# A hybrid retention and attention step: first loads into the key and score buffers, the last head's rows later, new delays

## The chip, the cores and the metric

The kernel runs on one core of one Trainium2 chip. The metric is the device time of one execution in microseconds (us); lower is better. The version before the change takes 669.69 us, the median of three runs (669.68, 669.69 and 672.77).

## The reference, cut to what matters

One step of a layer for 1024 prompt tokens and 64 sample tokens (the sample tokens have a cache of 128 keys and a running retention state), width 1024:

```python
h = rmsnorm(x, norm_g)
z = h @ w_in                        # 4096 columns: q, k, v, gate of 8 retention and 4 differential heads
o_ret  = retention(rotate(rq), rotate(rk), rv)       # per-token causal, a state per head
p = softmax(q_c @ k_c.T, masked)    # c = 0, 1, for each differential head, rotary on a part of q and k
o_diff = (p[0] - lam * p[1]) @ dv   # keys of the own and earlier 64-token chunks
mix = concat(rmsnorm(o_ret) * g * silu(rg), rmsnorm(o_diff) * g * (1 - lam0) * silu(dg))
y = final_rmsnorm(x + mix @ w_out)
# returned: y, the retention states, and k and v of the differential heads
```

## The kernel before, in words

**Tiles and groups.** The tokens are nine tiles: tiles 0 to 7 of 128 prompt tokens, tile 8 of 64 sample tokens. The input projection is cut into eight groups of 512 columns, in the order R0, D0, R1, D1, R2, D2, R3, D3: an R group holds q, k, v and gate of two retention heads, a D group those of one differential head. For each group, `proj` (L277) makes one 128x512 product `z` per tile; the first group takes tiles 0 to 3 together. Then `outproj` (L666) makes the two halves `zo0` and `zo1` of the output projection, tile by tile, adds x, and the final norm follows.

**Split precision.** x and the weights are each split in two parts, x = xh + xl and w = hi + lo. For each of the eight slices of 128 rows (k = 0 to 7) a tile takes three matmuls of 512 columns: xh with hi, xl with hi, xh with lo (tile 8: two). ScalarE writes the first part by a copy (`xh` L185, weights L138), VectorE the second by a subtraction (`xl` L186, weights L147). A weight slice lies in one of 12 slots (`WRING`, tag wsp), a raw one in one of 3 (`WRAW`, tag wraw), which the x rows for the norm (`xk`) and the rows of y share.

**How x comes in.** The transposed x of tiles 0 to 3 comes as eight slices `x0_k` of 256 KB, each for all four tiles (L226 to 232), through a ring of two buffers with the tag xraw; the loop asks for slice k, then has it split, so that SP, the DMA queue's engine, waits for a split before it asks for the slice after the next. Tiles 4 to 8 come as two halves each of 256 KB through the same ring (`load_x` L198, `prep_x` L205), each asked for and split while the group before that tile runs. `prep_ss` (L218) squares and sums the rows `xk` for the norm. Tag p is the ring of three 4 KB-wide score buffers of the differential heads; `khh` and `kll` hold a differential head's keys in two parts, and a differential head's first use of them is in the second group.

**What sets the order.** TensorE runs in the order in which the program emits it. A clock `clk.t` (in ns) adds up an estimate for each matmul. The steps after a projection (`diff_post` L328, `ret_post` L470) are generators that are cut into steps: each yield gives a delay (`D_QK`, `D_SPLIT`, ...), `HOLD[(group, tile, step)]` adds to it, and `pump` (L589) emits, after each k of a projection, the steps whose time `clk.t` has passed and whose buffers are counted free. `PACE_L` spaces the tiles of the last D group. The other engines' order is the scheduler's, which follows the order of the program and of what is ready. A D tile's steps: transposes `T`, the splits `qs`, `khh`, `kll`; scores `s` for c = 0, then 1 with row maxima `nm` (VectorE L410) and exponentials `p` (ScalarE L415); transposes `wt` of the combined weights and the copy `wT` (L444, L446), both for two halves of the keys where a tile has more than four blocks; the products `o`; a sum of squares (L181, L182, L462), the scaled product `mx` (VectorE L464); its transpose `mt` (L111); the copy `mix` (ScalarE L322). An R tile has `T`, the copies `rkT`, `rqT`, `qpad` (ScalarE L512), scores `s` and the masked `at` (VectorE L520), `o`, `mx` (VectorE L553), `mt`.

**The turn to the output projection.** Rows of groups 0 to 6 go to DRAM and come back (`prep_mix` L647, buffers `mraw`), three tiles ahead. The rows of the last group are split from `mix` itself by `prep_last` (L658), which forces all steps that are still missing for that tile. It is called one tile ahead: before the projection of tile i starts, the rows of tile i + 1 are forced out.

## Time and profile before

| | |
|---|---|
| median of the runs | 669.69 us |
| the profiled execution's own time | 671.67 us |
| its span in the trace | 669.9 us |
| granted TensorE clock, mean | 0.999 |
| TensorE matmuls busy | 649.4 us (97%) |
| VectorE busy | 462.9 us (69%) |
| ScalarE busy | 370.8 us (55%) |
| GpSimd busy | 91.2 us (14%) |

The span runs from the first to the last instruction that the profiler saw; 1.8 us of the execution's time lie outside it. PE is the matmul side of TensorE, PEld its weight loads, DVE is VectorE, ACT ScalarE, POOL GpSimd. In a timeline a row gives start, duration, engine, source line, operation, output <- inputs, shape, count, and in brackets the idle time of the engine just before it with the instruction whose end released it. Matmuls overlap, so a matmul's own duration is longer than the step from one start to the next. A row of the view by windows gives, for one stretch of time, the busy time of each engine.

### The profile page before, as it was taken

The numbers are of one execution on the slowest core, as the hardware profiler recorded it, in microseconds if no ns is written. First come the engines' busy times: TensorE is split into PE (matmuls) and PEld (weight loads), VectorE is DVE, ScalarE is ACT, GpSimd is POOL, SyncE is SP. The second block draws the span as 40 slices with busy tenths as digits, with TensorE's granted clock in tenths as the row PEclk, the third lists the DMA queues.
The fourth block names the chain that finished last, engine by engine and source line by source line (L and its number), as shares of the span: only waits on it lengthen the run. The fifth ranks groups of instructions, "written<-read, shape, count | busy, mean of one in ns | idle before, by whom it ended". The sixth has DMA issues, their size and how long they took to land.

```text
span 669.9 us, 10635 instructions
## 1 busy us (share of the span) xinstructions
PE 649.4 (97%) x3360; PEld 536.9 (80%) x3360; DVE 462.9 (69%) x1486; ACT 370.8 (55%) x1259; POOL 91.2 (14%) x194
## 2 busy tenths in 40 slices
PE   9989999999999999999999999999999998989996
PEld 7867878888888888788888788887887786778885
DVE  5487777797757566877676669766677788864533
ACT  6586565655546555654465557554655566742322
POOL 1222211001221011011111110111210100010000
PEclk9999999999999999999999999999999999999999
DMA  7973410230004101400022004000251025424464
GB/s 241 302 245 111 133 31 20 76 103 16 9 21 140 30 9 48 141 1 25 8 86 92 15 23 156 20 8 18 80 166 43 9 86 152 130 95 140 128 212 165
DMA packets 41192, 59.17 MB, mean 88 GB/s; under 512 B 6896, under 2 KB 25072, under 8 KB 41136
## 3 DMA queue, kind: packets, MB, share of 16 engines
q1 hardware_dynamic: 40848, 58.22, 27.4%
q8 instruction: 27, 0.44, 0.3%
q14 instruction: 29, 0.24, 0.1%
q10 hardware_dynamic: 288, 0.27, 0.1%
HBM read 42.91 MB, written 15.56 MB: 87 GB/s over the span
## 4 chain that ended last, share of the span: by engine, by line
PE 59%; DVE 16%; DMA 9%; ACT 8%; issue 4%; POOL 4%; SPq 0%; POOLq 0%; ACTq 0%; DVEq 0%
PE z L107 34%; PE zo L107 9%; PE s L107 8%; PE o L107 3%; POOL ss L182 3%; DMA wr<-in_wg 2%; DVE nm L410 2%; ACT p L415 2%; PE wt L111 2%; DMA x<-in_x 2%; PE T L111 2%; DVE kll L387 2%; DVE ws L147 1%; DVE xl L186 1%; DMA wr<-in_wo 1%
## 5 line engine op out<-in xcount | busy, mean ns | idle before, releaser
L107 PE MATMUL z<-ws,xh 128*128 128x512 f32 x1152 | 404.9, 409 | 0.5 <-ACT xh L185 0.5
L107 PEld LDWEIGHTS z<-ws,xh 128*128 128x128 f32 x1152 | 215.9, 189 | 41.1 <-ACT xh L185 1.0
L107 PE MATMUL z<-ws,xl 128*128 128x512 f32 x512 | 200.5, 392 | 0.4 <-DVE xl L186 0.4
L182 POOL TENSOR_TENSOR ss<-ss,m 128x2 f32<-128x2 f32 (+1 forms) x72 | 50.0, 694 | 459.6 <-DVE ss L181 453.3
L107 PEld LDWEIGHTS z<-ws,xl 128*128 128x128 f32 x512 | 97.0, 190 | 12.4 <-DVE xl L186 0.7
L415 ACT ACTIVATE p<-s,nm 128x384 f32<-128x384 f32 (+4 forms) x104 | 58.4, 565 | 73.0 <-DVE nm L410 41.6
L107 PE MATMUL zo<-ws,xh 128*128 128x512 f32 (+1 forms) x304 | 92.5, 384 | 0.0
L107 PEld LDWEIGHTS zo<-ws,xh 128*128 128x128 f32 x304 | 56.2, 189 | 10.3 <-ACT zo L693 0.2
L138 ACT ACTIVATE ws<-wr,early 128x512 fp32r<-128x512 f32 x80 | 54.2, 721 | 13.2 <-PE zo L107 4.6
L410 DVE TENSOR_REDUCE nm<-s 128x1 f32<-128x384 f32 (+4 forms) x104 | 55.7, 537 | 6.4 <-PE s L107 4.8
L147 DVE SCALAR_TENSOR_TENSOR ws<-wr,early,ws 128x512 fp32r<-128x512 f32 x80 | 57.6, 740 | 2.8 <-ACT ws L138 2.2
L387 DVE TENSOR_TENSOR kll<-T,khh 64x128 fp32r<-64x128 f32 (+1 forms) x144 | 40.3, 280 | 17.3 <-ACT khh L385 15.4
L107 PE MATMUL zo<-ws,xl 128*128 128x512 f32 (+1 forms) x136 | 51.3, 377 | 0.0
L107 PEld LDWEIGHTS o<-v,wT 128*128 128x128 f32 x288 | 39.1, 191 | 9.1 <-DVE mx L464 2.8
L107 PE MATMUL o<-v,wT 128*128 128x128 f32 x288 | 40.4, 276 | 3.3 <-DVE mx L464 2.4
L553 DVE SCALAR_TENSOR_TENSOR mx<-s,ss,gt 128x64 f32<-128x64 f32 x72 | 17.2, 280 | 35.7 <-POOL ss L549 35.6
L107 PE MATMUL s<-khh,qs 128*128 128x384 f32 (+4 forms) x104 | 36.8, 354 | 0.0
L107 PE MATMUL s<-kll,qs 128*128 128x384 f32 (+4 forms) x104 | 34.9, 339 | 0.3 <-DVE kll L387 0.2
L322 ACT ACTIVATE mix<-mt 128x128 f32<-128x128 f32 (+1 forms) x72 | 19.5, 271 | 25.7 <-PE mt L111 25.3
L384 ACT ACTIVATE khh<-T 64x128 fp32r<-64x128 f32 (+1 forms) x72 | 19.0, 264 | 25.3 <-DVE qs L382 24.8
L381 ACT ACTIVATE qs<-T 64x128 fp32r<-64x128 f32 x72 | 19.3, 268 | 24.8 <-DVE kll L387 15.4
L464 DVE SCALAR_TENSOR_TENSOR mx<-o,ss,gt 128x128 f32<-128x128 f32 x36 | 12.6, 351 | 27.3 <-POOL ss L462 27.1
(132 smaller groups left out, 965.6 us busy)
## 6 DMA issues: line engine op xcount, KB each, us to landing
wr<-in_wg SPq DMA_DIRECT2D x28, 512.0 KB, 4.5
xk<-in_xp SPq DMA_DIRECT2D x8, 512.0 KB, 5.7
wr<-in_wo SPq DMA_DIRECT2D x8, 512.0 KB, 4.4
y<-in_xp SPq DMA_DIRECT2D x16, 256.0 KB, 3.0
out_y<-y SPq DMA_DIRECT2D x15, 256.0 KB, 3.7
mixd<-mix SPq DMA_DIRECT2D x28, 128.0 KB, 1.7
x<-in_x SPq DMA_DIRECT2D x8, 256.0 KB, 4.2
wr<-in_wg SPq DMA_DIRECT2D x8, 256.0 KB, 3.8
```

What stands on the lines that cost most here:

```text
L107: pe.matmul(out, lhsT, rhs, start=start, stop=stop)
L111: pe.transpose(out, in_, ident)
L138: act.activation(s[:, 0, :], w, AF.Copy, scale=gain)
L147: dve.scalar_tensor_tensor(s[:, 1, :], w, gain, hi, ALU.mult, ALU.subtract)
L182: pool.tensor_tensor(out, out, m05[:rows, :n], ALU.pow)
L322: act.activation(mixbuf[g, c][:, off:off + rows], tp[:, :rows], AF.Copy)
L381: act.activation(qs[own, c], T[own, 0], AF.Copy, scale=0.125)
L384: act.activation(kc[own], T[own, 1, :rows], AF.Copy)
L387: dve.tensor_tensor(kll[half, c, o0:o0 + rows], T[own, 1, :rows], kc[own].bitcast(F32), ALU.subtract)
L410: dve.tensor_reduce(nm_[:, n, c:c + 1], sc[:, 0:b - a], AX.X, ALU.max, negate=True)
L415: act.activation(p[:, a:b], sc[:, 0:b - a], AF.Exp, bias=mx_, accum_out=zz[:, n, c:c + 1])
L553: dve.scalar_tensor_tensor(mx[:, sl], o[:, sl], ss[:, hh:hh + 1], gt[:, sl], ALU.mult, ALU.mult)
```

## The change

1. **The first x.** The eight slices `x0_k` go straight into two tiles with the tags khh and kll, which no head uses yet. All of them, the first group's weights, the whole of tiles 4, 5 and 6 and the rows `xk` 0 and 1 are asked for ahead of the loop of splits; no wait for a split lies between the slices.
2. **Later tiles.** `load_x` takes a whole tile (512 KB) into a buffer with the tag p. The splits of tiles 4 to 8 and the first `prep_ss` are emitted together when the first four tiles start. `WS_0` (the tile of the first group with which the next group's weight splits begin) goes from 5 to 4.
3. **The last head's rows.** `prep_last` is called inside `outproj(0, i)` before each k; it forces only from k = 6 (`KLAST`), and takes the next tile's rows early when they are done anyway.
4. **Delays.** The table `HOLD` has new and larger entries, among them 7.7 to 7.9 us for tiles 0 to 2 of the first group; `PACE_L` goes from 1000 to 1300; tile 8 of a D group may take its transposes with one step less behind the tile ahead.

```diff
--- before.py
+++ after.py
@@ -47,28 +47,37 @@
 PACE = 7000
 PACE_I = 1500
-PACE_L = 1000
+PACE_L = 1300
 HOLD = {
-    (0, 0, 1): 1658, (0, 0, 2): 1288, (0, 0, 3): 1174, (0, 1, 1): 1578, (0, 1, 2): 1158, (0, 1, 3): 1121,
...
+    (0, 0, 1): 2176, (0, 0, 2): 1629, (0, 0, 3): 7779, (0, 1, 1): 2146, (0, 1, 2): 7895, (0, 2, 1): 7692,
...
+    (7, 7, 7): 9669, (7, 8, 4): 11475, (7, 8, 5): 6942,
 }
+KLAST = 6
 WARM = 24
 POST0 = 6
@@ -83,7 +92,7 @@
 SPACE0 = 4000
 M_BUFS = 5
 N0 = 4
-WS_0 = 5
+WS_0 = 4
 WS_D = 2
 WS_R = 1
 GORDER = [("R", 0), ("D", 0), ("R", 1), ("D", 1), ("R", 2), ("D", 2), ("R", 3), ("D", 3)]
@@ -195,18 +204,17 @@
     xraw = {}
-    def load_x(i, half):
+    def load_x(i):
         n = 128 if i < 8 else NS
-        ks = slice(4 * half, 4 * half + 4)
-        xt = xp.tile([128, 4, 128], F32, tag="xraw", name=f"xraw{i}_{half}", bufs=2)
-        nc.sync.dma_start(xt[:, :, :n], I["xtp"][i - N0][:, ks] if i < 8 else I["xts"][:, ks])
-        xraw[i, half] = xt[:, :, :n]
+        xt = sp.tile([128, 8, 128], F32, tag="p", name=f"xraw{i}", bufs=PB)
+        nc.sync.dma_start(xt[:, :, :n], I["xtp"][i - N0] if i < 8 else I["xts"])
+        xraw[i] = xt[:, :, :n]
     def prep_x(i, half):
         hi, lo = x_hilo(i)
         ks = slice(4 * half, 4 * half + 4)
-        xt = xraw.pop((i, half))
-        split_x(hi[:, ks], lo[:, ks], xt)
+        split_x(hi[:, ks], lo[:, ks], xraw[i][:, ks])
     xtok = {}
@@ -223,23 +231,39 @@
         pool.tensor_scalar(rstdh[:rows, i:i + 1], rstd[:rows, i:i + 1], 0.5, None, ALU.mult)
+    x0t = [sp.tile([128, 4, N0, 128], F32, tag=t, name=f"x0{t}", bufs=1) for t in ("khh", "kll")]
+    late = cp.tile([128, 1144], F32, name="late")
+    def load_x0(k):
+        nc.sync.dma_start(x0t[k // 4][:, k % 4], I["x0"][:, k])
+    load_x0(0)
+    load_w(0, 0, 2)
+    load_x0(1)
+    load_w(0, 1, 2)
+    load_x0(2)
+    load_w(0, 2)
+    load_x0(3)
+    load_x0(4)
+    load_x0(5)
+    load_w(0, 3)
+    load_x0(6)
+    load_x0(7)
+    load_x(N0)
+    load_ss(0)
+    nc.sync.dma_start(late, I["late"])
+    load_x(N0 + 1)
+    load_ss(1)
+    load_x(N0 + 2)
     for k in range(KD):
-        xt = xp.tile([128, N0, 128], F32, tag="xraw", name=f"x0_{k}", bufs=2)
-        nc.sync.dma_start(xt, I["x0"][:, k])
-        if k % 2 == 0:
-            load_w(0, k // 2, 2)
         split_w_hi(0, k)
-        split_x(xh[:, 0:N0, k], xl[:, 0:N0, k], xt)
+        split_x(xh[:, 0:N0, k], xl[:, 0:N0, k], x0t[k // 4][:, k % 4])
         split_w_lo(0, k)
     ident = cp.tile([128, 128], F32, name="ident")
     make_identity(nc, ident)
-    late = cp.tile([128, 1144], F32, name="late")
-    load_ss(0)
-    nc.sync.dma_start(late, I["late"])
-    for half in range(2):
-        load_x(N0, half)
-    for i in range(1, N0):
+    for i in range(2, N0):
         load_ss(i)
     rcs = late[:, 0:864].rearrange("p (t a d) -> p t a d", t=9, a=3)
     dec = late[:, 864:880].rearrange("p (a b) -> p a b", a=4)
@@ -590,7 +614,9 @@
         prev, ready = {}, []
         for e in list(live):
-            if e[1] < prev.get(e[4], 1 << 30) and all(free[k] >= v for k, v in e[3].items()):
+            ahead = 2 if e[4] == "D" and e[5] == 8 and e[1] == 0 else 0
+            if e[1] + ahead < prev.get(e[4], 1 << 30) and all(free[k] >= v for k, v in e[3].items()):
                 if force:
                     ready.append(e)
                 elif due(e) <= clk.t:
@@ -655,7 +681,13 @@
             nc.sync.dma_start(m[:, 0:ng_, :rows], src)
             split_x(hi[:, 4 * half:4 * half + ng_], lo[:, 4 * half:4 * half + ng_], m[:, 0:ng_, :rows])
-    def prep_last(i):
+    lasts = set()
+    def prep_last(i, force=True):
+        if i in lasts or i > 8 or not force and (7, i) not in done:
+            return
+        lasts.add(i)
         while (7, i) not in done:
             start_posts()
             pump(True)
@@ -676,6 +708,10 @@
         for hf, (a, b) in enumerate(halves):
             z = ps.tile([128, 512], F32, tag="z", name=f"zo{n}_{i}_{hf}", bufs=2)
             for k in range(8):
+                if n == 0:
+                    prep_last(i, k >= KLAST)
+                    if i in lasts:
+                        prep_last(i + 1, False)
                 w = wsp[8 + n, k]
                 seq = [(xh, 0), (xl, 0), (xh, 1)] if i < 8 else [(xh, 0), (xh, 1)]
                 for q_, (xx, wi) in enumerate(seq):
@@ -711,16 +747,17 @@
         for tiles in ([list(range(N0))] if g == 0 else [[i] for i in range(N0)]) + [[i] for i in range(N0, 9)]:
             i = tiles[-1]
             if g == 0:
-                nxt = [i + 1, i + 2] if i == N0 - 1 else [i + 2]
-                for t in nxt:
-                    if t < 9:
+                if i == N0 - 1:
+                    for t in range(N0, 9):
+                        if t > N0 + 2:
+                            load_x(t)
                         for half in range(2):
-                            if t > N0:
-                                load_x(t, half)
                             prep_x(t, half)
+                        if t - N0 < 4:
+                            prep_ss(t - N0)
                         load_ss(t)
-                for t in tiles:
-                    prep_ss(t)
+                else:
+                    prep_ss(i)
             lead = WS_0 if g == 0 else WS_D if kind == "D" else WS_R
             for kk in range(4):
                 if i == (lead + 2 * kk - 1 if kk < 2 else 5 + kk):
@@ -744,14 +781,11 @@
         start_posts()
         pump(True)
     nc.sync.dma_start(late[:, 0:1024], I["fng"])
-    prep_last(0)
     for n in range(2):
         for j, i in enumerate(first if n == 0 else [0, 8] + list(range(1, 8))):
             if n == 0:
                 if j + MIXA < 9:
                     prep_mix(first[j + MIXA])
-                if j + 1 < 9:
-                    prep_last(first[j + 1])
                 if 4 <= j < 8:
                     split_w(9, j - 4)
                 if j in (3, 5, 7, 8):
```

**Place 1: ScalarE at the start**, where the first group's splits of x end (`xraw4`, `xraw5` are x of tiles 4 and 5, `xk` the squares for the norm, `rv0` and `th` the first steps after a projection). Before:

```order
L185 ACTIVATE xh_112<-xraw4_0_191 128x512
L221 ACTIVATE xk2_197,ssx_76<-xk2_197 128x1024
L185 ACTIVATE xh_112<-xraw4_1_193 128x512
L221 ACTIVATE xk3_199,ssx_76<-xk3_199 128x1024
L492 ACTIVATE rv0_358<-z0_0_257,rstd_74 128x128
L261 ACTIVATE ls_209<-ls_209 128x2
L307 ACTIVATE th0_0_361<-z0_0_257,rstdh_75 128x128
L492 ACTIVATE rv0_358<-z0_1_258,rstd_74 128x128
L307 ACTIVATE th0_1_420<-z0_1_258,rstdh_75 128x128
L221 ACTIVATE xk4_229,ssx_76<-xk4_229 128x1024
L185 ACTIVATE xh_112<-xraw5_0_231 128x512
L185 ACTIVATE xh_112<-xraw5_1_235 128x512
```

With the change:

```order
L194 ACTIVATE xh_112<-x0kll_115 128x4x128 x2
L194 ACTIVATE xh_112<-xraw4_135 128x512 x2
L229 ACTIVATE xk0_137,ssx_76<-xk0_137 128x1024
L194 ACTIVATE xh_112<-xraw5_140 128x512 x2
L229 ACTIVATE xk1_142,ssx_76<-xk1_142 128x1024
L194 ACTIVATE xh_112<-xraw6_144 128x512 x2
L516 ACTIVATE rv0_372<-z0_0_271,rstd_74 128x128
L331 ACTIVATE th0_0_375<-z0_0_271,rstdh_75 128x128
L229 ACTIVATE xk2_191,ssx_76<-xk2_191 128x1024
```

The splits of tiles 4, 5 and 6 now stand ahead of the first projection's own steps; before, the second half of tile 4 came just ahead of them, and tile 5 after those of tiles 0 and 1.

**Place 2: VectorE ahead of `mx7_4`**, the last step on VectorE of the last head's tile 4, during `zo0_0` and `zo0_1`. Before:

```order
L696 TENSOR_TENSOR y0_0_6697<-y0_0_6697,late_187 128x512
L382 SCALAR_TENSOR_TENSOR qs7_6_6716<-T7_6_6713,qs7_6_6716 64x128
L181 TENSOR_SCALAR ss7_4_6771<-ss7_4_6771 128x1
L444 COPY wT7_5_0_6780<-wt7_5_0_6779 128x384
L387 TENSOR_TENSOR kll3_5939<-T7_6_6713,khh3_5938 64x128 x2
L186 TENSOR_TENSOR xl_113<-mraw4_0_6753,xh_112 128x512
L186 TENSOR_TENSOR xl_113<-mraw4_1_6757,xh_112 128x384
L464 SCALAR_TENSOR_TENSOR mx7_4_6777<-o7_4_6709,ss7_4_6771,gt7_4_6295 128x128
L410 TENSOR_REDUCE nm7_6_6792<-s7_6_0_0_6794 128x1
```

With the change:

```order
L190 TENSOR_SCALAR ss7_4_6771<-ss7_4_6771 128x1
L728 TENSOR_TENSOR y0_1_6718<-zo0_1_0_6720,y0_1_6718 128x512
L411 TENSOR_TENSOR kll3_5921<-T7_6_6733,khh3_5920 64x128 x2
L488 SCALAR_TENSOR_TENSOR mx7_4_6777<-o7_4_6726,ss7_4_6771,gt7_4_6277 128x128
L732 TENSOR_TENSOR y0_1_6718<-y0_1_6718,late_116 128x512
L195 TENSOR_TENSOR xl_113<-mraw5_0_6792,xh_112 128x512
L195 TENSOR_TENSOR xl_113<-mraw5_1_6796,xh_112 128x384
```

The splits of the reloaded rows (`mraw`, L186 before and L195 after) stood between the sum of squares `ss7_4` and `mx7_4`; now they stand behind `mx7_4`, and a sum of 512 columns for y stands there.

**Place 3: tiles 7 and 8 of the last head.** TensorE with the change, from tile 7's second product to its transpose `mt7_7`:

```order
L116 MATMUL o7_7_7171<-v3_5919,wT7_7_1_7193 128x128 x4
L120 MATMUL wt7_8_0_7235<-ident_186,p7_8_0_7156 128x128 x2
L116 MATMUL zo0_7_0_7210<-ws8_4_6580,xh_112 128x512
L116 MATMUL zo0_7_0_7210<-ws8_4_6580,xl_113 128x512
L116 MATMUL zo0_7_0_7210<-ws8_4_6580,xh_112 128x512
L116 MATMUL zo0_7_0_7210<-ws8_5_6585,xh_112 128x512
L116 MATMUL zo0_7_0_7210<-ws8_5_6585,xl_113 128x512
L116 MATMUL zo0_7_0_7210<-ws8_5_6585,xh_112 128x512
L120 MATMUL mt7_7_7246<-ident_186,mx7_7_7233 128x128
```

Six matmuls of 512 columns and one `wt` of tile 8 lie between tile 7's last product and its `mt`; before there were nine in the place of the six. ScalarE around tile 8's `mix` (that is `mix7_4`, 64 columns) before:

```order
L322 ACTIVATE mix7_4_7256<-mt7_8_7254 128x64
L185 ACTIVATE xh_112<-mix7_4_7256 128x64
L693 ACTIVATE zo0_6_0_7214,yss_224<-y0_6_7212 128x512
L138 ACTIVATE ws9_4_7303<-wr9_2_7263,early_79 128x512
L693 ACTIVATE zo0_7_0_7267,yss_224<-y0_7_7265 128x512
L138 ACTIVATE ws9_5_7308<-wr9_2_7263,early_79 128x512
L138 ACTIVATE ws9_6_7313<-wr9_3_7296,early_79 128x512
L138 ACTIVATE ws9_7_7318<-wr9_3_7296,early_79 128x512
L689 ACTIVATE zs8_0_7329<-zo0_8_0_7300 64x512
```

With the change:

```order
L194 ACTIVATE xh_112<-mix7_3_7152 128x128
L484 ACTIVATE junk7_8_7258,ss7_8_7257<-o7_8_7254,rz7_8_7185 128x128
L147 ACTIVATE ws9_4_7279<-wr9_2_7206,early_79 128x512
L729 ACTIVATE zo0_7_0_7210,yss_218<-y0_7_7208 128x512
L147 ACTIVATE ws9_5_7284<-wr9_2_7206,early_79 128x512
L147 ACTIVATE ws9_6_7289<-wr9_3_7272,early_79 128x512
L147 ACTIVATE ws9_7_7294<-wr9_3_7272,early_79 128x512
L346 ACTIVATE mix7_4_7303<-mt7_8_7301 128x64
L194 ACTIVATE xh_112<-mix7_4_7303 128x64
L725 ACTIVATE zs8_0_7311<-zo0_8_0_7276 64x512
```

The copy `mix` of tile 8 and the split `xh` of it move from ahead of the four weight splits `ws9_4` to `ws9_7` to behind them. These splits write slots that the projection of tile 8, `zo0_8`, frees as it goes.

## Rows read from the trace of the kernel before

**Rows 1.** The page's busy times of each engine over the span.

```profile
PE 649.4 (97%) x3360; PEld 536.9 (80%) x3360; DVE 462.9 (69%) x1486; ACT 370.8 (55%) x1259; POOL 91.2 (14%) x194
```

**Rows 2.** Windows: stretch, length, PE, PEld, DVE, ACT, POOL, PEclk, DMA, GB/s.

```profile
28.00:60.00 32.00, 28.81 (x141) 22.74 (x140) 25.37 (x79) 24.06 (x75) 10.56 (x21) 1.00 0.74 234
240.00:290.00 50.00, 48.74 (x246) 39.46 (x246) 38.68 (x127) 29.38 (x97) 3.56 (x8) 1.00 0.21 65
455.00:465.00 10.00, 9.03 (x51) 6.99 (x50) 6.51 (x23) 4.96 (x20) 0.99 (x2) 1.00 0.10 29
505.00:541.00 36.00, 34.78 (x177) 28.20 (x176) 26.43 (x102) 21.27 (x78) 3.84 (x8) 1.00 0.04 11
541.00:560.00 19.00, 18.54 (x93) 14.87 (x91) 16.14 (x49) 13.46 (x40) 1.33 (x3) 1.00 0.41 125
560.00:580.00 20.00, 17.25 (x91) 14.12 (x90) 17.71 (x45) 12.68 (x37) 1.02 (x3) 1.00 0.46 135
580.00:595.00 15.00, 12.62 (x72) 10.48 (x71) 12.20 (x32) 9.09 (x31) 1.04 (x3) 1.00 0.40 125
595.00:609.00 14.00, 14.00 (x70) 11.46 (x69) 5.20 (x14) 3.73 (x13) 1.78 (x4) 1.00 0.27 92
```

**Rows 3.** Timeline of PE: five of the eighteen pauses over 0.15 us.

```profile
34.50 0.50 PE L107 MATMUL z<-ws,xh 128*128 128x512 f32 x1 [0.54 <-ACT xh L185]
...
44.32 0.66 PE L107 MATMUL s<-rv,at 128*128 128x64 f32 x4 [1.16 <-DVE at L520]
...
508.65 0.41 PE L111 MATMUL T<-ident,qk 128*128 128x128 f32 x2 [1.10 <-DVE rz L424]
...
562.13 0.30 PE L111 MATMUL mt<-ident,mx 128*128 128x128 f32 x1 [1.82 <-DVE mx L464]
...
591.82 1.16 PE L107 MATMUL o<-v,wT 128*128 128x128 f32 x8 [2.38 <-DVE mx L464]
```

**Rows 4.** Chain of waits, an unbroken stretch of PE; and its group of the page.

```profile
606.72 50.89 PE zo L107 x224
...
L107 PE MATMUL zo<-ws,xh 128*128 128x512 f32 (+1 forms) x304 | 92.5, 384 | 0.0
```

**Rows 5.** Windows at the start, and DMA issues from 0 to 60 us.

```profile
0.00:6.00 6.00, 4.88 (x23) 3.48 (x24) 1.44 (x2) 3.50 (x5) 2.98 (x16) 1.00 0.65 201
20.00:25.00 5.00, 5.00 (x24) 4.14 (x23) 1.39 (x2) 1.82 (x3) 0.72 (x2) 1.00 0.87 278
30.00:35.00 5.00, 4.46 (x20) 2.99 (x18) 4.83 (x17) 4.59 (x12) 2.66 (x8) 1.00 0.93 315
...
xk<-in_xp SPq DMA_DIRECT2D x8, 512.0 KB, 5.7
...
xraw<-in_xtp SPq DMA_DIRECT2D x8, 256.0 KB, 3.9
```

**Rows 6.** Timeline of DVE ahead of `mx` of the last head's tile 4.

```profile
560.44 1.16 DVE L186 TENSOR_TENSOR xl<-mraw,xh 128x512 fp32r<-128x512 f32 x2
561.63 0.35 DVE L464 SCALAR_TENSOR_TENSOR mx<-o,ss,gt 128x128 f32<-128x128 f32 x1
```

**Rows 7.** Timeline of PE and DVE: tile 7's last product, `mx` and `mt`.

```profile
597.04 1.06 PE L107 MATMUL o<-v,wT 128*128 128x128 f32 x8
...
599.95 0.35 DVE L464 SCALAR_TENSOR_TENSOR mx<-o,ss,gt 128x128 f32<-128x128 f32 x1 [1.11 <-POOL ss L462]
...
600.36 0.33 PE L111 MATMUL mt<-ident,mx 128*128 128x128 f32 x1
```

**Rows 8.** Timeline of ACT and DVE: weight splits around tile 8's split of `mix`.

```profile
612.70 0.73 ACT L138 ACTIVATE ws<-wr,early 128x512 fp32r<-128x512 f32 x1 [4.60 <-PE zo L107]
613.94 1.94 ACT L138 ACTIVATE ws<-wr,early 128x512 fp32r<-128x512 f32 x3
...
607.30 0.23 DVE L186 TENSOR_TENSOR xh<-mix,xh 128x64 fp32r<-128x64 f32 x1
614.69 2.08 DVE L147 SCALAR_TENSOR_TENSOR ws<-wr,early,ws 128x512 fp32r<-128x512 f32 x3 [0.36 <-ACT ws L138]
```

40 rows, old and new, of the table HOLD are left out of this document.

## The prediction

> **What bounds the kernel now.** I read the busy times first: TensorE's matmuls fill 97% of the span, and no other engine is over 69% [rows 1]. So time can come only from the places where TensorE pauses, or runs off its best pace. The change issues the same matmuls, so its whole effect is on pauses.
>
> The windows say where these are [rows 2]. In most of the span TensorE loses a few tenths of a microsecond in 10 us. It loses more in 28 to 60 us (32.00 − 28.81 = 3.19 us), 240 to 290 (1.26), 455 to 465 (0.97), 505 to 541 (1.22), 541 to 560 (0.46), 560 to 580 (2.75) and 580 to 595 (2.38). The sum is 12.23 us, 1.8% of the span. From 595 us on to the last output-projection matmul there is nothing to gain: 595 to 609 has 14.00 busy in 14.00. The clock granted is 1.00 in every window shown.
>
> The timeline of PE then names each pause, five of eighteen shown [rows 3]: a projection's matmul that waits for a split of x (34.50), a retention product that waits for `at` (44.32), transposes that wait for ScalarE and VectorE to free or fill a buffer (508.65), and, in the last head, steps behind `mx` (562.13: 1.82 us; 591.82: 2.38 us).
>
> A pause costs more than its idle time. Unbroken, 224 matmuls take 50.89 us, 0.227 us each, while one is busy for 384 ns on average [rows 4]: its end overlaps the next one. A pause loses that overlap too, 384 − 227 = about 0.16 us. I price each pause at idle + 0.16 us. The profiled execution took 671.67 us, 1.98 over the median 669.69; I sum against 671.67 and take 1.98 off at the end.
>
> **The change, part by part.** Three questions decide each pause: which instruction it waits for, how many matmuls now lie between the producer and the consumer, and what stands on the other engines between. The counts come from the order of the changed kernel; 0.227 us for each 512-column matmul.
>
> *First loads and the start, 28 to 60 us.* Now: 3.19 us idle and five pauses, 3.19 + 5 × 0.16 = 4.0. The two waits for tile 5's split (34.50 and the one behind it) had a transfer and a ring of two buffers ahead of them. With all loads asked for at once, what must land up to tile 6 is 2 MiB of first slices, 2 of weights, 1.5 of tiles 4 to 6, 1 of `xk` and 0.56 of tables: 7.4 MB. At 201 GB/s in the first 6 us (1.2 MB) and about 290 after (between 278 and 315) [rows 5], it has landed by 6 + 6.2 MB / 290 GB/s = 27.4 us; TensorE wants tile 5 at 34.50 − 0.54 − 0.16 = 33.8. The first four slices have about 2 us of slack by the same rates. So these waits go. What covers the splits: they stand ahead of the first heads' steps on ScalarE (place 1), which the new 7.8 us delays make wait anyway. The wait for `at` of tile 1 (1.16) does not vanish: three fewer matmuls lie ahead (0.68 us less), and weight splits, begun a tile earlier, can stand before it. I leave 1.3 us here for that kind. **Gain 2.7**; ends: 4.0 if nothing is left, 1.0 if two more waits like the one at 44.32 appear (2 × (1.16 + 0.16) = 2.6, less 1.3 already counted, and some 0.4 of slips).
>
> The whole-tile loads cost something too: a 512 KB transfer took 5.7 us to land and one of 256 KB 3.9 [rows 5], so a tile's first half comes up to 1.8 us later. The 6.4 us of slack for tile 5 cover it; without that cover it is 1.8 us. The Trainium skill, page "Perfetto Trace Analysis", section "DMA Optimizations", speaks against this step: smaller pieces may let some work start sooner where DMA engines are generally idle. The trace does not meet its condition: the DMA share is 0.87 and 0.93 in these windows [rows 5]. By that rule the time would be 1.8 us more than my sum, which stays inside the forecast.
>
> *Delays in groups 1 to 6.* 240 to 290: four pauses, 1.26 + 4 × 0.16 = 1.9. Tile 4's first product `o` gets six matmuls more (1.4 us, more than its 0.56 wait), its second none, and the first tiles of that group get less. **Gain 0.9** (ends 0 and 1.9). 455 to 465: 0.97 + 3 × 0.16 = 1.45; the transpose of `mx` gets 1.7 us more and the scores 1.4, against waits of at most 0.51. **Gain 1.1** (ends 0 and 1.45). 505 to 541: 1.22 + 2 × 0.16 = 1.5, nearly all of it the transposes at 508.65, whose distance is the same as before. **Gain 0.2** (ends −0.3 and 1.5).
>
> *The last head, 541 to 595 us.* Five pauses: 0.46 + 2.75 + 2.38 + 5 × 0.16 = 6.4. Tile 4's `mt` (562.13, 1.82 us) waited for `mx`, and two splits of reloaded rows, 1.16 us, ran right ahead of that `mx` [rows 6]. They now stand behind it (place 2), and the distance has three matmuls more (0.68): 1.84 against 1.82, about 0.1 left. Tile 5's `mt` keeps its distance: 0.5 left. The wait at 591.82 hangs on the ring of `o`: tile 7's product cannot start until tile 6's `mx` has read it. Its distance grows by some nine matmuls, 2.1 us: 0.4 left. The small waits around 542 and 557: 0.5.
>
> Two new waits come. Tile 7: `o` ends at 598.10 and `mt` starts at 600.36 without a pause, so the steps between need 2.26 us [rows 7]. Nine matmuls and a transposition covered that; now six do (place 3), 6 × 0.227 + 0.14 = 1.50: a pause of 0.75. Tile 8: its `mix` copy and split now stand on ScalarE and VectorE behind `ws9_4` to `ws9_7` (place 3). These wait for slots that `zo0_8` frees: the first ran at 612.70, the last ended on ScalarE at 615.88, on VectorE at 616.77; then comes the 0.23 us split, 617.0 [rows 8]. `zo0_8` began at about 612.2, and its k = 7 is 14 matmuls later, 612.2 + 3.2 + 0.1 = 615.5. A pause of 1.5, ahead of the last two matmuls of tile 8. Nobody else waits for it: the second half's first weights are in place.
>
> Left: 0.1 + 0.5 + 0.4 + 0.5 + 0.75 + 1.5 = 3.75, of which the tile-7 pause can hide up to 0.35 of the rest, since all behind it arrives earlier: 3.4. **Gain 3.0**; ends 6.4 (both new waits absent) and 0 (each of six remaining waits 0.5 larger).
>
> *The cover for the later last rows.* Tile 8's transposes move 39 matmuls (8.9 us) later, so the head's steps run where VectorE was busy for 5.20 of 14.00 us (595 to 609) instead of 16.14 of 19.00, 17.71 of 20.00 and 12.20 of 15.00 (541 to 595) [rows 2]. The tail behind `zo1` is untouched: 0.
>
> **Sum.** 2.7 + 0.9 + 1.1 + 0.2 + 3.0 = 7.9; 671.67 − 7.9 = 663.8, and less 1.98, 661.8: I say **662.0**. A difference of 0.5% is 3.35 us, about the least that a measurement of this kernel can tell from none: faster is under 666.3, slower over 673.0.
>
> **The rivals.**
>
> *B. Nearly all pauses go.* 12.23 us + 20 × 0.16 = 15.5: 671.67 − 15.5 − 1.98 = 654.2. For it: each delay is put where a wait was. Against: T of tile 2 keeps its distance, and the two new waits are in the order. Chance 0.08.
>
> *C. The change does not do what it says.* A forced step ignores its delay: tile 0's last step in the first group, delayed by 7.8 us, keeps its distance (6.30 us before, 6.27 now), since buffers ran out and forced it. If most steps are forced likewise, and only half of the start's gain and that of 240 to 290 us come, I get 1.3 + 0.9 = 2.2: 669.69 − 2.2 = 667.5. For it: a step also waits until its few buffers are counted free. Against: most distances did grow. Chance 0.15.
>
> *D. Slower: the last head's steps crowd the end.* Forced at k = 6 of the tile that wants them, the 18 steps between `zo0_4` and `zo0_8` each wait on a chain of VectorE and ScalarE. Before, the five pauses were 6.4 us over 18 steps, 0.36 each. If each now waits 0.9 us, 18 × 0.9 = 16.2, less the old 6.4 and the 4.9 gained elsewhere: 669.69 + 4.9 = 674.6. It decides from 0.8 us per step on. For it: VectorE was 85% busy from 541 to 595 (46.05 of 54.00) [rows 2]. Against: it was 37% busy from 595 to 609, and 8.9 us of that come into use. Chance 0.05.
>
> **How the numbers follow.** Forecast (657 to 666.3): 0.72. B below 657: 0.08. C, 666.3 to 673: 0.15. D: 0.05. Faster is the forecast and B, 0.80; same 0.15; slower 0.05. The forecast's ends: 661.8 − 4.7 with the favourable ends of the two larger terms (4.0 − 2.7 = 1.3 and 6.4 − 3.0 = 3.4), and 661.8 + 4.7 with their unfavourable ones (2.7 − 1.0 = 1.7 and 3.0), cut at the 0.5% bound. The range, 657 to 668, takes in most of C, and leaves out B, D and the rest of C, under 0.2.
>
> **What would show it.** Right: no wait of a projection's matmul for `xh` or `xl` around 34 us; 44's wait for `at` not over 1.2; around tile 4's `mt` no wait over 0.5; the transposes of tile 2 in the last head still pausing for about 1.1; a pause of 0.75 ahead of tile 7's `mt` and of 1.5 in tile 8's k = 7, on a split that stands behind weight splits; idle of PE in the seven windows down from 12.2 to 6 to 7 us. Wrong: new pauses over 1 us in the first 28 us (slices late), or many of 0.5 to 1 us in 560 to 609, VectorE at over 90% there. If the pauses go as named and the time does not, then the price of 0.16 a pause, or the pace, was wrong.

## The result, and the profile after

The changed kernel takes **659.5 us** (median of four runs, 659.09 to 660.16), the kernel before 670.96 us beside it: ratio 0.9824, 95% interval 0.9809 to 0.9840. That is 11.5 us or 1.8% less. The forecast was 662.0 us and faster, so the sign and the range held; the gain was half as large again as the 7.9 us of the sum. The profiled execution took 660.16 us, with a span of 658.4.

The page's busy times after the change; the row before is [rows 1].

```profile
PE 645.6 (98%) x3360; PEld 538.5 (82%) x3360; DVE 460.4 (70%) x1486; ACT 369.3 (56%) x1259; POOL 91.4 (14%) x194
```

TensorE's idle time fell from 669.9 − 649.4 = 20.5 us to 658.4 − 645.6 = 12.8 us, and its busy time by 3.8 us for the same matmuls. In both kernels about 7.6 us of the idle time lie ahead of the first matmul (1.1) and behind the last (6.5), so between them it fell from 12.8 to 5.2 us. I read both falls as the pauses: 7.7 us that they show as idle, and the overlap of neighbouring matmuls that each of them, and each slip too short to be listed, had cost.

The windows of the changed kernel, with the columns of [rows 2]. Everything comes some microseconds earlier than in [rows 2], so the windows of the last head cover slightly later work.

```profile
0.00:28.00 28.00, 26.30 (x117) 20.59 (x118) 14.50 (x24) 17.63 (x30) 4.59 (x20) 1.00 0.91 331
28.00:60.00 32.00, 32.00 (x167) 27.05 (x166) 24.11 (x82) 23.95 (x81) 12.15 (x24) 1.00 0.58 174
...
240.00:290.00 50.00, 50.00 (x262) 42.40 (x262) 38.73 (x129) 29.35 (x99) 5.03 (x10) 1.00 0.20 65
...
455.00:505.00 50.00, 49.31 (x260) 40.55 (x259) 34.68 (x119) 29.26 (x107) 7.32 (x14) 1.00 0.32 98
505.00:541.00 36.00, 36.00 (x184) 30.10 (x184) 26.58 (x95) 21.36 (x73) 3.58 (x8) 1.00 0.12 39
541.00:560.00 19.00, 18.89 (x97) 15.51 (x96) 16.68 (x48) 12.09 (x34) 0.89 (x2) 1.00 0.52 158
560.00:580.00 20.00, 19.63 (x99) 15.78 (x98) 17.14 (x42) 14.03 (x41) 1.28 (x3) 1.00 0.47 141
580.00:595.00 15.00, 15.00 (x86) 12.82 (x85) 9.04 (x27) 6.41 (x25) 0.90 (x2) 1.00 0.32 109
595.00:609.00 14.00, 11.72 (x54) 9.14 (x53) 7.34 (x16) 5.91 (x15) 1.78 (x4) 1.00 0.36 116
```

28 to 60 and 240 to 290 us have no idle time left, 541 to 595 only 0.48 us of the former 5.59. More than half of the 5.2 us that are left between the first and the last matmul sits at two places: the first 28 us (1.70 us idle, 1.12 of them ahead of the first matmul in both kernels) and 595 to 609 us (2.28 us). The timeline of PE in the changed kernel shows the pauses there, and the one that I expected to stay around 508:

```profile
9.16 0.50 PE L116 MATMUL z<-ws,xh 128*128 128x512 f32 x1 [0.35 <-ACT xh L194]
9.89 0.50 PE L116 MATMUL z<-ws,xl 128*128 128x512 f32 x1 [0.22 <-DVE xl L195]
...
500.63 0.41 PE L120 MATMUL T<-ident,qk 128*128 128x128 f32 x2 [0.33 <-DVE rz L448]
...
596.59 0.33 PE L120 MATMUL mt<-ident,mx 128*128 128x128 f32 x1 [0.66 <-DVE mx L488]
603.69 0.50 PE L116 MATMUL zo<-ws,xh 128*128 128x512 f32 x1 [1.62 <-DVE xh L195]
```

The two new waits of the last head are there at the sizes forecast: tile 7's `mt` 0.66 us (forecast 0.75), tile 8's last slice 1.62 (1.5). The waits at 9 to 10 us were not forecast. In the seven windows that the prediction adds up, 0.48 us idle are left where it expected 6 to 7; the two new pauses now fall behind them, in 595 to 609.

Where the time came from is best read from the starts of the same product in both traces. The lead is how much earlier the changed kernel is:

| first matmul of | before | after | lead | growth | forecast |
|---|---|---|---|---|---|
| first group, tile 0 | 6.08 | 5.75 | 0.33 | | |
| first group, tile 4 | 28.07 | 28.85 | −0.78 | −1.1 | 0 |
| second group | 67.05 | 63.68 | 3.37 | +4.15 | 2.7 |
| fourth group | 206.37 | 202.10 | 4.27 | +0.9 | 0 |
| sixth group | 344.88 | 339.01 | 5.87 | +1.6 | 0.9 |
| seventh group | 405.58 | 399.39 | 6.19 | +0.3 | 0 |
| eighth group (last head) | 482.69 | 474.73 | 7.96 | +1.8 | 1.1 |
| second half of the output projection | 615.67 | 604.26 | 11.41 | +3.45 | 3.2 |

A single step of this table is known to about 1 us. Kernels 3, 4 and 5 below run the program of before up to the second group, and begin that group at 66.91, 65.98 and 66.56 us instead of 67.05; the changed kernel begins it at 63.81 in a second profile (kernel 12).

### The profile page after: what moved, and what is told of

Read it like the earlier page. It is cut to its first block, busy times and chain, and to the rows that moved or that the text cites. A ratio compares the mean times of both kernels' runs of the same rounds, so it can differ in the third digit from the quotient of the medians.

```text
span 658.4 us, 10628 instructions
## 1 busy us (share of the span) xinstructions
PE 645.6 (98%) x3360; PEld 538.5 (82%) x3360; DVE 460.4 (70%) x1486; ACT 369.3 (56%) x1259; POOL 91.4 (14%) x194
## 4 chain that ended last, share of the span: by engine, by line
PE 81%; DVE 7%; DMA 5%; ACT 2%; issue 2%; POOL 2%; SPq 0%; POOLq 0%; ACTq 0%; DVEq 0%
PE z L116 51%; PE s L116 10%; PE zo L116 10%; PE o L116 5%; PE wt L120 3%; DMA mraw<-mixd 3%; DVE ws L156 2%; PE T L120 2%; POOL ss L191 1%; PE mt L120 1%; DMA x0khh<-in_x 1%; ACT xh L194 1%; DMA wr<-in_wo 1%; DVE xl L195 1%; ACT p L439 0%
## 5 line engine op out<-in xcount | busy, mean ns | idle before, releaser
L452 DVE SCALAR_TENSOR_TENSOR p<-p,rz,p 128x384 f32<-128x384 f32 (+4 forms) x52 | 29.8, 599 | 0.5
```

Source lines behind the costliest of these rows:

```text
L452: dve.scalar_tensor_tensor(wt[:, a:b], P[1][:, a:b], rz[:, 2:3], P[0][:, a:b], ALU.mult, ALU.add)
```

## The experiments

The first five kernels take the change apart on the kernel before, the sixth takes one part out of the changed kernel, 7 to 11 mend what the trace of the changed kernel shows, and 12 is the changed kernel once more.

**1. The loads alone.** Parts 1 and 2 on the kernel before:

```diff
-PACE_L = 1300
+PACE_L = 1000
 HOLD = {
...
-                if n == 0:
-                    prep_last(i, k >= KLAST)
-                    if i in lasts:
-                        prep_last(i + 1, False)
```

(as a difference from the changed kernel; `HOLD`, `prep_last` and the rule for tile 8 are those of before.)

> Only parts 1 and 2: the first x goes into the key buffers, later tiles whole into the score buffers, WS_0 is 4; delays and last rows as before. My theory: the two waits for tile 5's split around 34.5 us go (0.90 us idle, 1.2 with the overlap), but the first four tiles end later than before, since each slice now shares the queue with those asked for behind it (0.77 us later in the changed kernel), and the waits for at and qpad at 44 to 58 us stay, as they belong to the delays: 0.3 to 1.0 us less than before, 669 to 670.5 us beside a before of 671. Rival: the loads bring the whole gain of the start, then the second group begins 3.4 us earlier and the time is 667.5.

Measured 667.07 us, ratio 0.9942 (0.9920 to 0.9964): the rival, 3.9 us. The second group begins 4.4 us earlier than before, more than in the changed kernel, and without a single new delay. The wait for `at` at 44 us is gone too, which I had given to the delays. And though the loads are those of the changed kernel, there is no pause near 9 us here: slice 1 landed at 7.55 us, and the first four tiles took 22.27 us (from tile 0's first matmul to tile 4's), against 22.00 before and 23.11 in the changed kernel. The last head's pauses are all as before, so the loads have no part in that. The timeline of PE in this kernel:

```profile
556.51 0.30 PE L109 MATMUL mt<-ident,mx 128*128 128x128 f32 x1 [1.80 <-DVE mx L477]
...
573.02 0.33 PE L109 MATMUL mt<-ident,mx 128*128 128x128 f32 x1 [0.84 <-DVE wT L457]
...
586.21 1.05 PE L105 MATMUL o<-v,wT 128*128 128x128 f32 x7 [2.47 <-DVE mx L477]
```

**2. Loads and the first group's delays.** As 1, with the entries (0, ...) of the new `HOLD`.

> Parts 1 and 2 with the new delays of the first group alone; the delays of the other groups and the last rows as before. My theory: the gain of the start is loads and these delays together, the second group begins 3.4 us earlier than before and nothing is given back later: 667.5 us beside a before of 671. Rival: the later delays are fitted to the new start, so with the old ones about 1.5 us come back as waits in groups 1 to 3: 669.

Measured 667.88 us, ratio 0.9955 (0.9939 to 0.9970). The size is near the first theory's, but its reason fell: with the delays the second group begins 3.85 us earlier, without them 4.38. The delays give nothing beside the loads. Here too no pause stands near 9 us (slice 1 landed at 7.19 us).

**3. The delays of groups 1 to 6 alone.** The entries (1, ...) to (6, ...) of the new `HOLD` in the kernel before.

> Only the new delays of groups 1 to 6; loads, last rows and the other delays as before. My theory: the parts add up. In the changed kernel the lead over before grows by 4.6 us from the second group's first projection to the last group's, and the loads alone already bring 0.6 of that, so these delays alone bring 4.0 us: 667.3 us beside a before of 671.3, and the last head unchanged. Rival: they are fitted to the earlier start of the changed kernel and bring under 2 us with the old one: above 669.3.

Measured 667.98 us beside 672.31, ratio 0.9947 (0.9926 to 0.9968): 3.6 us, near the 4.0 of the theory. From 240 to 300 us no pause over 0.15 us is left; the start and the last head wait as before, but for one pause of the last head's transposes, which fell from 1.10 to 0.34 us (PE):

```profile
504.31 0.41 PE L114 MATMUL T<-ident,qk 128*128 128x128 f32 x2 [0.34 <-DVE rz L427]
```

**4. The last rows asked for later, alone.** `prep_last` inside `outproj` with `KLAST = 6`, everything else as before.

> Only part 3: the last head's rows are forced from k = 6 of their own tile on; all delays, PACE_L and the loads as before. My theory: the later demand gives the last head's steps more matmuls to hide behind by itself, and takes about half of the 6.4 us of pauses between 541 and 595 us: 668 us beside a before of 671. Rival: the gain there is the delays', and without them the steps come at the same places or are waited for at k = 6: within 0.7 us of before, 670.5 to 671.5.

Measured 670.57 us beside 671.26, ratio 0.9988 (0.9970 to 1.0007): the rival. Its lead does not grow in the last head (1.86 us at the last tile's projection, 1.91 at the second half). The pauses stay, in the timeline of PE:

```profile
560.32 0.30 PE L112 MATMUL mt<-ident,mx 128*128 128x128 f32 x1 [1.77 <-DVE mx L465]
...
577.05 0.33 PE L112 MATMUL mt<-ident,mx 128*128 128x128 f32 x1 [1.10 <-DVE wT L445]
...
590.23 0.94 PE L108 MATMUL o<-v,wT 128*128 128x128 f32 x6 [1.75 <-DVE mx L465]
...
613.18 0.98 PE L108 MATMUL zo<-ws,xh 128*128 128x512 f32 x3 [0.23 <-DVE xh L187]
```

So asking later does not move the steps by itself; with the delays, `PACE_L` and the rule for tile 8 they move (kernel 5). Whether those would do it without the later asking was not run.

**5. The last head alone.** As 4, with `PACE_L = 1300`, the entries (7, ...) of the new `HOLD` and the rule for tile 8.

> Part 3 with all that belongs to the last head: its delays, PACE_L 1300, the earlier transposes of tile 8. Loads and the delays of the other groups as before. My theory: stages are independent, and the last head alone brings what the changed kernel gained from the start of its projection on, 3.4 us, the new pause of 1.6 us ahead of tile 8's last slice included: 667.5 us beside a before of 671. Rival: the last head only gains because groups 0 to 6 leave its engines less work behind; then under 2 us: 669 to 670.

Measured 666.88 us, ratio 0.9944 (0.9920 to 0.9968): 3.8 us, the first theory. The waits of 1.8 and 2.4 us are gone; the two new ones of the changed kernel are there, at the same sizes (PE):

```profile
602.98 0.33 PE L110 MATMUL mt<-ident,mx 128*128 128x128 f32 x1 [0.67 <-DVE mx L463]
...
610.08 0.97 PE L106 MATMUL zo<-ws,xh 128*128 128x512 f32 x3 [1.63 <-DVE xh L185]
```

Kernels 1, 3 and 5 take 0.58, 0.53 and 0.56% off, 1.67% in sum; all together take 1.76% (1.60 to 1.91). Within their noise (about 0.2% each) the parts add up. Kernels 4 and 5 change nothing between the second and the eighth group, and still lead by 0.85 to 1.0 us more there, mostly in the seventh group: that is the profiled execution of before, not the change. Of the 1.8 us in the table's seventh-group step some 0.65 are of this kind.

**6. The changed kernel with the first group's old delays.**

> The changed kernel with the first group's delays of before (the 7.7 to 7.9 us among them gone). My theory, from the loads alone, which gained as much without these delays as with them: they bring nothing, 659.0 to 659.5 us where the changed kernel takes 659.5, and the second group begins 0.5 us earlier than with them. Rival: the delays of group 1 are fitted to them; then 0.7 us or more come back as waits in groups 1 and 2: 660.2 or more.

Measured 659.69 us (659.09 to 660.15), the changed kernel 659.5. The delays of 7.7 to 7.9 us change nothing in the time that can be measured: without them the second group begins 0.5 us earlier, and by the fourth the two kernels are within 0.1 us.

**7. Tile 8's end.** The last head's rows are split from the transposed product itself, tile 8's are forced at k = 4, and two weight splits are emitted later:

```diff
+        if g == 7:
+            hi, lo = x_hilo(i)
+            split_x(hi[:, 7], lo[:, 7], tp[:, :rows])
+            done.add((g, i))
+            rel("mx")
+            return
...
-                    prep_last(i, k >= KLAST)
+                    prep_last(i, k >= (KLAST8 if i == 8 else KLAST))
...
-                if i == first[8] and n == 0 and k < 4:
+                if i == first[8] and n == 0 and k < 2:
                     split_w(9, k + 4)
+                if i == 0 and n == 1 and k < 2:
+                    split_w(9, k + 6)
```

> The changed kernel with the last head's rows split straight from the transposed product in PSUM (no copy between), tile 8's forced from k = 4 of its projection on, and two of the four weight splits for the second half emitted behind it. My theory: the 1.62 us pause ahead of tile 8's last slice is the queue of weight splits on ScalarE and VectorE, so it goes, 1.8 us with the overlap: 657.7 us where the changed kernel takes 659.5; tile 7's pause of 0.66 stays. Rival: the chain from mx to the split is itself too long, or the weight splits now come late for the second half; then under 0.7 us: above 658.8.

Measured 659.59 us (659.04 to 659.81): no gain, yet not by the rival's mechanism. The pause did shrink from 1.62 to 0.34 us, and from the first matmul of the output projection to that of its second half this profile takes 66.07 us, against 67.15 and 66.67 in the two profiles of the changed kernel. Part of it was given back at a new place, in the timeline of PE:

```profile
551.61 0.55 PE L121 MATMUL wt<-ident,p 128*128 128x128 f32 x3 [0.48 <-DVE p L459]
...
603.18 0.98 PE L117 MATMUL zo<-ws,xh 128*128 128x512 f32 x3 [0.34 <-DVE xh L196]
```

The transposes of tile 5 now wait for combining p, since VectorE splits the rows of the earlier tiles at other places of its queue (kernel 11, which leaves these splits where they were, has no such wait). And in this profile the first slices came later still (a wait of 1.06 us at 9.81 us), so that tile 4 began 0.65 us later than in the changed kernel. Why none of the other three runs is faster either, one profile does not show.

**8. Tile 7 as well.** `(7, 7, 4): 0`, `(7, 8, 3): -1000`, `(7, 8, 4): 11100`, `(7, 8, 5): 12000` in the table of kernel 7.

> As the kernel before this one, and with other delays for tiles 7 and 8 of the last head, so that 12 instead of 6 matmuls lie between tile 7's last product and its transpose. My theory: the 0.66 us pause there is distance alone and goes, 0.8 us more with the overlap: 656.9 us. Rival: tile 7's first product, now earlier, waits for the buffer that tile 6's mx reads, and the pause moves there: the same as the kernel before, within 0.3 us.

Measured 658.07 us (657.24 to 658.51), 1.5 us less than kernel 7. Tile 7's pause is gone, and its first product does not wait. Of the 0.7 us beyond the 0.8 expected no cause in tile 7 shows; the two profiles differ by 0.6 us in the first 28 us, where both run the same program, so the first slices' landing times alone can move a kernel by that much.

**9. The start.** The changed kernel, but slices 0 to 2 go through the ring of two buffers, and slice 2 with all behind it is asked for once slice 0 is split:

```diff
+        x0[k] = x0t[k // 4][:, k % 4] if k >= 3 else xp.tile([128, N0, 128], F32, tag="xraw", name=f"x0_{k}", bufs=2)
...
     for k in range(KD):
...
+        if k == 0:
+            load_x0(2)
+            load_w(0, 2)
+            load_x0(3)
...
```

> The changed kernel, but the first three slices of x go through the ring of two buffers again, so that the third and all behind it are asked for only once the first is split. My theory: in the changed kernel the second slice was asked for as early as before, yet landed 1.4 us later, since the slices asked for behind it share the queue's bandwidth; that costs the first four tiles about 1 us, which nothing gives back. So the second slice is there by about 7.5 us again, the waits at 9.2 and 9.9 us go, and the time is 658.5 to 658.8 us where the changed kernel takes 659.5. Rival: the third and fourth slices, now later, are waited for instead, or tile 4's x is late: the same time as the changed kernel within 0.4 us.

Measured 658.36 us (657.69 to 658.82), 1.1 us less than the changed kernel, with no overlap of the runs (on another chip; the ratio to the kernel before there, 0.9782 with 0.9760 to 0.9803, does not overlap the changed kernel's either). Tile 4 begins 0.46 us before the kernel before instead of 0.78 behind it. Slice 1 is asked for at 2.1 us in all three kernels; the split of it on ScalarE, in the kernel before, the changed kernel and this one:

```profile
7.06 0.63 ACT L185 ACTIVATE xh<-x 128x512 fp32r<-128x512 f32 x1 [1.00 <-DMA x<-in_x]
```

```profile
8.48 0.63 ACT L194 ACTIVATE xh<-x0khh 128x512 fp32r<-128x512 f32 x1 [2.15 <-DMA x0khh<-in_x]
```

```profile
6.74 0.63 ACT L194 ACTIVATE xh<-x 128x512 fp32r<-128x512 f32 x1 [0.39 <-DMA x<-in_x]
```

**10. Start and ends together.** The start of 9 in kernel 8.

> The same start, put into the kernel with the mended ends of tiles 7 and 8 (658.07 us). My theory: the places are far apart and add up: 657.1 us. Rival: as the kernel before this one, no gain from the start: 658.

Measured **657.64 us** (657.32 to 658.08), ratio 0.9769 (0.9747 to 0.9790) to the kernel before. Its runs lie below all runs of the changed kernel: 1.9 us or 0.3% better than that, the best that was run. The sum would have been 657.0. But the runs of this kernel and of kernel 8 (657.24 to 658.51) overlap, so that the start brings something on top of kernel 8 is not shown by the times. In its profile the start brought 0.65 us of kernel 9's 1.24: slice 1 landed at 7.83 us, and tile 4 begins 0.18 us behind the kernel before.

**11. The straight split for tiles 7 and 8 alone.** As 10, with `if g == 7 and i >= 7`.

> The start of the third slice on request, and the mended ends of tiles 7 and 8, but with the straight split from PSUM for these two tiles alone, so that VectorE keeps the changed kernel's order for tiles 0 to 6. My theory: in the kernel that joined start and ends, the straight splits of tiles 1 to 6 pushed in front of combining p and cost about 1 us between 541 and 600 us; without that the gains of start (1.1 us), tile 7 (0.8) and tile 8 (1.3) add up: 656.3 us. Rival: the 1 us was lost elsewhere, by the earlier steps of tile 7, and stays: 657.3 to 657.7 us.

Measured 658.19 us (657.00 to 658.54), above both the 656.3 us of the theory and its rival. Kernel 10's two waits ahead of tile 5's transposes (0.49 and 0.34 us) are gone, as expected; a wait of 0.21 us for p is left ahead of tile 6's, where kernel 12 has one of 0.15. But a pause came to the place that kernel 8's rival had named, tile 7's first product, though for another reason than the one given there. The timelines of PE and DVE:

```profile
585.85 1.16 PE L114 MATMUL o<-v,wT 128*128 128x128 f32 x8 [1.23 <-DVE wT L475]
```

```profile
573.98 0.29 DVE L193 TENSOR_TENSOR xl<-mix,xh 128x128 fp32r<-128x128 f32 x1 [1.51 <-ACT xh L192]
...
585.11 0.69 DVE L475 COPY wT<-wt 128x512 f32<-128x512 f32 x1
```

Tile 7's first product stands six matmuls earlier than in kernel 9, as it does in kernel 10, and waits for its copy `wT`. VectorE runs that copy behind tile 8's key splits and a sum for y in both kernels; in kernel 10 it comes at 584.21 us, ahead of a product at 585.21. What differs is that VectorE runs late here: at 573.98 it waits 1.51 us for ScalarE, which splits a tile's rows from their copy `mix` behind two operations that waited 1.05 and 1.02 us for transfers. In kernel 10 the straight split at 572.38 did not wait. So the straight splits of the earlier tiles may also have kept VectorE ahead of tile 7; how much of this is the program, and how much the transfers of this one execution, is open. A delay between those of 9 and 11 for this one step was not tried.

**12. The changed kernel again**, on the chip of 11.

> The changed kernel as it is, beside the kernel before this one on the same chip: 659.5 us by all theories, within 0.5.

Measured 659.53 us (659.23 to 660.47), ratio 0.9825 (0.9809 to 0.9841).

## Why the prediction was right, and where its sizes were off

**What bounds the kernel: right.** No work left TensorE, and its pauses account for the gain. The price of idle + 0.16 us holds: the pause of 1.62 us at 603.69 costs 1.79 us (2.02 us from one start to the next, where 0.227 is the rule). What the count of pauses left out are slips under 0.15 us each. The pauses over 0.15 us behind the first matmul fell from 18 with 12.4 us to 9 with 4.5 us; at 0.16 us more for each that is 9.4 of the 11.5 us between the two spans. The other 2.1 us, in steps that are too short to be listed, no row of mine carried.

**What was luck.** The sum missed by 3.6 us (11.5 measured, 7.9 forecast), and the number by only 2.5: I took 1.98 us off for the profiled execution, and against the 670.96 us of the four runs it is 0.7. And the start came out near its forecast in sum, 4.15 − 1.1 = 3.05 us beside 2.7, by two errors of opposite sign, which follow.

**The start, 2.7 forecast for 28 to 60 us: too small, and one step of it wrong.** "I leave 1.3 us here for that kind" rested on `at` of the second tile, which does stand behind weight splits. The wait at 44.32 [rows 3] was for `at` of the first tile. In the kernel before, it stood on VectorE behind a weight split that waited for ScalarE, which waited for a weight transfer. The timelines of ACT and DVE before:

```profile
42.42 1.33 ACT L138 ACTIVATE ws<-wr,early 128x512 fp32r<-128x512 f32 x2 [1.30 <-DMA wr<-in_wg]
...
43.18 0.75 DVE L147 SCALAR_TENSOR_TENSOR ws<-wr,early,ws 128x512 fp32r<-128x512 f32 x1 [1.17 <-ACT ws L138]
43.85 0.42 DVE L520 TENSOR_TENSOR at<-s,late 128x256 f32<-128x256 f32 x1
```

In the changed kernel it stands ahead of the second group's weight splits and runs 3.8 us ahead of its matmul. DVE and PE:

```profile
39.85 0.42 DVE L544 TENSOR_TENSOR at<-s,late 128x256 f32<-128x256 f32 x1
...
43.61 0.55 PE L116 MATMUL s<-rv,at 128*128 128x64 f32 x4
```

So nothing was left of the 4.0 us. That it is the loads and the new order of the splits, not the delays, kernels 1, 2 and 6 show.

**"The first four slices have about 2 us of slack": wrong.** I worked with the rate of the first 6 us [rows 5] as if each transfer ran alone in its turn. Slice 1 landed 6.36 us after it was asked for, the first link of the chain of waits of the changed kernel:

```profile
2.10 6.36 DMA x0khh<-in_x
9.89 23.89 PE z L116 x104
```

This cost 1.1 us in this profile that the forecast did not have; kernel 9 gets it back. It is not the same in each execution: with the same loads slice 1 landed between 7.19 (kernel 2) and 9.11 us (kernel 7), and the first four tiles took 22.3 us in kernels 1 and 2 and 22.8 to 23.8 in the five others. With the loads of before it landed between 6.18 and 7.04, and they took 21.9 to 22.2 (four profiles). The Trainium skill's rule on splitting transfers ("Perfetto Trace Analysis", section "DMA Optimizations") was not what decided: from tile 4 on no matmul waited for a split of x, and the loss was among slices that were as small as before.

**Groups 1 to 6: sizes.** The table's 0.9 us from the second group to the fourth were forecast at 0. Kernel 3 gains 0.3 us there, and so does kernel 6; most of the rest is the 0.5 us that the first group's delays had cost before the second group (kernel 6). My counts of pauses in 240 to 290, 455 to 465 and 505 to 541 (4, 3 and 2) are each one more than the trace has over 0.15 us, 0.5 us in all of what could be gained. I left 1.0 of 1.9 us in 240 to 290 us; nothing is left, and kernel 3 shows that the delays do it alone. The 1.1 us before the last head were right once the 0.65 us of the profiled execution are taken off. "Nearly all of it the transposes at 508.65, whose distance is the same as before" failed: the wait fell from 1.10 to 0.33 us at the same distance. The profile names the same releaser on VectorE, `rz`, before and after, so it came earlier there. It is the delays of groups 1 to 6 that move it: with them alone the wait is 0.34 us (kernel 3), with those of the last head alone 1.03 (kernel 5). Which of them does it was not followed. A distance counted on TensorE is only half of a wait.

**The last head, 3.2 forecast, 3.45 measured: right**, with both new pauses. Three small leftovers of the forecast (0.5, 0.4 and 0.5 us) appear only as waits of at most 0.22 us.

**The rivals.** D, the crowd at the end, did not come: 541 to 595 us has 0.48 us idle. C named the delays of the first group as forced and so without effect. That they bring no time kernel 6 shows; that they are without effect it does not, since with them the second group begins 0.5 us later. B was nearer than its chance of 0.08 says: 11.5 us lie halfway between the sum's 7.9 and B's 15.5. The two new pauses, which spoke against it, came, and with the first slices' waits they are 2.9 of the 5.2 us that are left.

## What to carry to other kernels

Follow each pause to the queue in which its producer stands, and ask what stands ahead of it there and what that waits for; on VectorE a cheap operation behind a split that waits for a transfer was worth 1.3 us. Changing when something is demanded moves nothing by itself; it is the steps' own times that must move (kernel 4 against 5). Ask early for what is needed late, but only after what is needed first has landed. And compare a pause near a transfer over several profiles before giving it a price: the same loads made none in two kernels and over 1 us in another.

## What the hardware showed that I had not expected

A transfer landed later when more was asked for right behind it. From 0 to 40 us the issues of slices (256 KB each; the last number is the median time from issue to landing in us), in the kernel before, the changed kernel, and kernel 9, whose first three slices have the name x:

```profile
x<-in_x SPq DMA_DIRECT2D x8, 256.0 KB, 4.2
```

```profile
x0khh<-in_x SPq DMA_DIRECT2D x4, 256.0 KB, 6.6
...
x0kll<-in_x SPq DMA_DIRECT2D x4, 256.0 KB, 7.1
```

```profile
x0kll<-in_x SPq DMA_DIRECT2D x4, 256.0 KB, 8.4
...
x<-in_x SPq DMA_DIRECT2D x3, 256.0 KB, 3.5
```

More requests at once moved more in all, 331 GB/s over the first 28 us in the changed kernel (its first window above) against 261 before, but the slice that was needed next came 1.4 us later. Kernel 9 moved 327 GB/s and had it at 6.72 us. The other profiles vary a good deal: slice 1 landed between 6.18 and 7.04 us with the loads of before (4 profiles), 7.19 and 9.11 with all asked for at once (7), and 6.72 and 7.83 with the rest held back (3), which overlaps both. On one chip, kernels 3, 6, 7 and 8 have 6.18 against 8.45, 9.11 and 8.53; on another, kernels 4, 5, 1 and 2 have 6.60 and 6.93 against 7.55 and 7.19.

That the requests share the bandwidth evenly is not what the traces show. A landing is told there by sixteen updates of a semaphore, and the transfer has landed with the last. For slice 1 the eighth came at 5.83 us in the kernel before, 5.84 in the changed kernel and 5.75 in kernel 9; the last came at 7.04, 8.46 and 6.72. So half of the slice was reported as early in all three, and the loss is in the last few updates. Why these are late when more is asked for behind was not tested.
